# Moving the first head group's delta rule three steps later in a four-layer hybrid block

## The chip, the cores and the metric

One core of one Trainium2 chip runs the whole program once. The metric is device time in microseconds (us), from the host's request to its end; the profile's span runs from the first to the last instruction and is about 2 us shorter.

## The reference

Four layers over x of 256 tokens by 1024 channels, in fp32. Layers 1 and 2 are attention layers that the change doesn't touch. Layers 3 and 4 (`layer2` in the kernel) each do this, cut to what matters:

```
proj = rmsnorm(x) @ w_in            # q, k, v, z, b, a of the delta branch; q, k, v of the window branch; two gates
q, k, v = split(silu(conv4(q, k, v)))      # causal convolution over 4 tokens: the "taps"
q, k = l2norm(q) / sqrt(128), l2norm(k)    # 8 heads of 128
o = gated_delta_rule(q, k, v, g, beta)     # per head and chunk: a unit lower triangular solve
y_a = (rmsnorm(o) * silu(z)) @ w_up_dn
y_b = swa_sink(q, k, v) @ w_up_sw          # 16 heads, window of 128, sinks
x = x + rmsnorm((sigmoid(gate_a) * y_a + sigmoid(gate_b) * y_b) @ w_o)
x = x + rmsnorm(relu(rmsnorm(x) @ w_ff1)^2 @ w_ff2)
```

## The kernel before

**Projections.** TensorE (PE) multiplies in a split form: every weight piece `raw` (two rows of 128 input channels, 512 columns, 512 KB) is loaded by SyncE's queue (SP), copied by ScalarE (ACT) into `hi` (L290), and VectorE (DVE) writes the rest, `lo = raw - hi` (L291). Three matmuls per 128 channels then use hi and lo. `proj` (L318 to L320) makes token-major results, `proj_w` (L359 to L361) channel-major ones. Four split pieces and three raw ones are held; a piece's split is issued a half step after the piece four before it has been used, and the next raw load right behind it.

**The clock in the source.** Everything else is put between the matmuls by a clock that is written out by hand: `at(k, fn)` files work k steps ahead, and `tick(0.5)` after each half step first feeds a split and then issues what is due. A step is 128 input channels, so a projection of four pieces is 8 steps. Each engine then runs its own instructions in the order of issue.

**The delta branch in `layer2`.** The 8 heads are done in two groups `hh` of 4. Per group: `dn_qk` projects q and k (two `proj_w`), `dn_rest` files the delta rule, then come the gate's projection and that of v; the second group's q and k follow those, and then its own `dn_rest`, with the window branch (`swa`) between. Each convolution is filed by `into_conv`: ACT multiplies by one tap (L1001), DVE adds the three others with six instructions (L1004, "taps"), ACT takes tanh (L1008), DVE forms the silu (`emit`, L1021 for q and k, L1053 for v). For q and k, ACT squares it (L1029) and PE sums over channels into `pn` (L1027); for v PE transposes it (L1059) and DVE scales it into R (L1061).

**The delta rule as `dn_rest` files it**, from `start`, counted from the call:

- `decay_rows` at start - 3.2: a DMA on SP reads the decay sums `rw` from DRAM, spread over 128 partitions (512 KB, L1068).
- per head i, 2 steps apart from start - 1.5: `steps` (DVE, D from rw, L1074), exp and weigh (ACT, L1087, L1092), two `gram`s at start + 1.5 and + 1.7 (PE into a PSUM tile, L1096 and L1097; DVE multiplies by D, L1098), `pick` (POOL, L1113).
- at start + 9.5 `compact` (DVE, L1121); the 16x16 diagonal blocks go to DRAM and back in another layout (two DMAs on SP).
- at start + 15.1 to 18.1 the substitution on 64 partitions: two `eights` (DVE, L1149 and L1151), two `corner`s (DVE, L1164 and L1166, then L1159 and L1162); two DMAs again.
- at start + 21.7 and 22.7 `spread(1)` and `spread(0)` (DVE, L1169) make Xi, at start + 24.7 the doubling levels begin (`level_z` L1178, `level_y` L1188, `flip` L1107), then `solve`, `right` and `outputs`, the last at start + 41.8.

Grams, transposes, levels and the window branch's scores share three PSUM tiles of the tag `wk`; each is free again when ACT or DVE has read it. Each engine's queue keeps its order, so an instruction that waits holds up what is behind it.

Of the kernel before, what the change touches and what calls it, by code (L numbers as in the profile page):

```python
# [77 lines left out]
def body(ctx: ExitStack, tc: tile.TileContext, I, out, upto=None):  # L78
# [148 lines left out]
    clk = [0.0]  # L227
# [122 lines left out]
    def proj_w(lh, evac):  # L350

        acc = acc2()
        for c in range(8):
            if c % 2 == 0:
                hi, lo, n = piece()
            for m in range(4):
                a = acc[m // 2][:, (m % 2) * 256:(m % 2) * 256 + 256]
                sl = slice(m * 128, (m + 1) * 128)
                T.matmul(a, hi[:, c % 2, sl], lh[0][:, c, :], start=(c == 0 and m % 2 == 0), stop=False)  # L359
                T.matmul(a, hi[:, c % 2, sl], lh[1][:, c, :], start=False, stop=False)  # L360
                T.matmul(a, lo[:, c % 2, sl], lh[0][:, c, :], start=False, stop=(c == 7 and m % 2 == 1))  # L361
                if m == 3 and c % 2:
                    release()
                if m % 2:
                    if c == 7:
                        evac(acc[m // 2], m // 2)
                    tick(0.5)
# [518 lines left out]
    def layer2(l, last):  # L886
# [101 lines left out]
        def into_conv(m0, emit):  # L988

            def evac(acc, b):  # L990
                a = acc.rearrange("p (m t) -> p m t", m=2)
                w = cw[l]
                ha, hb = [sm.tile([128, 2, 256], F32, name="hcv", tag="hcv", bufs=4) for _ in range(2)]

                def tap(j, m):
                    c = 24 * j + m0 + 2 * b + m
                    return w[:, c:c + 1]

                def taps():
                    for m in range(2):  # L1000
                        S.activation(ha[:, m, :], a[:, m, :], AF.Copy, scale=tap(3, m))  # L1001
                    for d in (1, 2, 3):
                        for m in range(2):
                            V.scalar_tensor_tensor(ha[:, m, d:], a[:, m, :256 - d], tap(3 - d, m), ha[:, m, d:],  # L1004
                                                   op0=ALU.mult, op1=ALU.add)

                def silu():
                    S.activation(hb, ha, AF.Tanh)  # L1008

                for k, fn in ((0.4, taps), (4.2, silu), ((4.9, 4.7)[m0 // 4 % 2], lambda: emit(b, hb, ha))):  # L1010
                    at(k + b, fn)
            return evac

        def dn_qk(hh):
            dqk = qk_tile([2, 4, 256])
            dq, dk = dqk[:, 0], dqk[:, 1]
            pn = wk([128, 2, 2, 4], "pn", "o", 1)
            for qi, d in enumerate((dq, dk)):
                def emit(b, th, hcv, d=d, qi=qi):
                    x = d[:, 2 * b:2 * b + 2, :]  # L1020
                    V.scalar_tensor_tensor(x, th, 1.0, hcv, op0=ALU.add, op1=ALU.mult)  # L1021
                    sq = th

                    def norms():
                        for m in range(2):
                            for t in range(2):
                                T.matmul(pn[:, qi, t, 2 * b + m:2 * b + m + 1], sq[:, m, t * 128:(t + 1) * 128], ones,  # L1027
                                         start=True, stop=True)
                    at(1.1, lambda: S.activation(sq, x, AF.Square))  # L1029
                    at(3.4, norms)  # L1030
                proj_w(lh, into_conv(8 * qi + 4 * hh, emit))
            return dq, dk, pn
# [299 lines left out]
        m1, fins, end = [], [], 0.0  # L1332

        def gate(g):
            m1.append(t4k("tg"))
            proj(lh, into_tanh(m1[g], None))
# [3 lines left out]
        def swa(g):  # L1340
            q = qk_tile([8, 256], F32R)
            if g == 0:
                sw["lb"] = new_lh()
            y, evac = into_stack(q, None, rope2)
            proj(lh, evac)
            windowed(q, g, y)

        for hh in range(2):
            qkn = dn_qk(hh)
            emit_v, fin, end = dn_rest(hh, *qkn, max(10.5, end + -15.3 - clk[0]))  # L1350
            fins.append(fin)
            if hh:
                swa(0)
            gate(hh)
            if hh:
                swa(1)
            proj_w(lh, into_conv(16 + 4 * hh, emit_v))
# [169 lines left out]
    at(67.3, lambda: tab_load("bs", "nb16"))  # L1527
    at(8.9, vectors)
    steps = [layer1, layer1, layer2, layer2][:upto]
    for i, s in enumerate(steps):  # L1530
        s(i % 2, i == len(steps) - 1)
# [27 lines left out]
```

## Time and profile before

| | |
|---|---|
| median of 3 runs | 1730.53 us (1729.9 to 1733.3) |
| the profiled execution's own time | 1731.44 us |
| its span | 1729.5 us |
| mean granted TensorE clock | 0.995 of full speed |
| TensorE busy | 1699.3 us of the span (98%) |
| VectorE busy | 1171.5 us (68%) |
| ScalarE busy | 1000.7 us (58%) |

The time outside the span is 1.9 us. TensorE is busy nearly throughout, so the time is its work plus the stretches in which it stands. Shares over the whole span hide that these stretches stand close together; stages have to be read one by one.

### The profile page before, as it was taken

Reading aid. Unit: us, or ns where it says so; the run is one execution under the profiler, and the core shown is the slowest. Engines: PE = TensorE matmul, PEld = TensorE weight load, DVE = VectorE, ACT = ScalarE, POOL = GpSimd, SP = SyncE. Lnnn points to the kernel's source line nnn. Section 1 sums busy time; section 2 is a strip of 40 time slices with the busy share of each in tenths; the row PEclk is TensorE's granted clock in tenths of the full one; section 3 lists DMA queues with packets and bytes.
Section 4 is the critical chain, followed back from the end, with each engine's and each line's share of the span. In section 5 each row is a group of like instructions: output and inputs, shape, how many; then the busy total and the mean of one; then the engine's idle time right before and its main releaser. Section 6 shows DMA issues by size and latency. Waiting matters only on the chain.

```text
span 1729.5 us, 26895 instructions
## 1 busy us (share of the span) xinstructions
PE 1699.3 (98%) x9865; PEld 1482.8 (86%) x9865; DVE 1171.5 (68%) x2206; ACT 1000.7 (58%) x1787; POOL 259.4 (15%) x491
## 2 busy tenths in 40 slices
PE   9999999999999999998999999999999999999998
PEld 7788888888888888898898889998998898889997
DVE  6676866666678756878685676556778584775554
ACT  6666665466667554665676465445665666464443
POOL 1112320021123200420210000000320211010000
PEclk9999999999999999999999999999999999999999
DMA  6666465566555565555242546665554333556554
GB/s 220 192 177 177 153 186 162 173 197 178 169 171 166 164 195 170 165 167 143 83 117 86 195 158 187 191 195 172 164 166 140 88 103 98 195 160 199 183 182 142
DMA packets 158948, 282.27 MB, mean 163 GB/s; under 512 B 20576, under 2 KB 28512, under 8 KB 158816
## 3 DMA queue, kind: packets, MB, share of 16 engines
q1 hardware_dynamic: 157712, 277.57, 53.3%
q0 software_dynamic: 720, 2.62, 0.4%
q8 instruction: 78, 1.28, 0.3%
q14 instruction: 54, 0.44, 0.1%
q10 hardware_dynamic: 384, 0.35, 0.1%
HBM read 270.53 MB, written 1.59 MB: 157 GB/s over the span
## 4 chain that ended last, share of the span: by engine, by line
PE 49%; DVE 6%; issue 1%; ACT 1%; DMA 0%; POOL 0%; DVEq 0%; POOLq 0%; ACTq 0%
PE acc L320 6%; PE acc L318 6%; PE acc L319 6%; PE acc L359 5%; PE acc L360 4%; PE acc L361 4%; PE facc L318 3%; PE facc L319 3%; PE facc L320 3%; DVE lo L291 2%; DVE hcv L1004 1%; PE inv L1188 1%; PE inv L1178 1%; PE tp L377 1%; PE pg L1096 1%
## 5 line engine op out<-in xcount | busy, mean ns | idle before, releaser
L291 DVE TENSOR_TENSOR lo<-raw,hi 128x1024 fp32r<-128x1024 f32 (+2 forms) x505 | 617.0, 1228 | 367.8 <-ACT hi L290 354.6
L290 ACT ACTIVATE hi<-raw 128x1024 fp32r<-128x1024 f32 (+2 forms) x505 | 528.4, 1052 | 370.0 <-PE acc L320 158.6
L318 PE MATMUL acc<-hi,lhi 128*128 128x512 f32 (+1 forms) x1344 | 550.0, 409 | 1.3 <-ACT hi L290 1.3
L320 PE MATMUL acc<-hi,llo 128*128 128x512 f32 (+1 forms) x1344 | 525.4, 391 | 0.4 <-DVE llo L394 0.3
L319 PE MATMUL acc<-lo,lhi 128*128 128x512 f32 (+1 forms) x1344 | 523.9, 390 | 0.8 <-DVE lo L291 0.7
L320 PEld LDWEIGHTS acc<-hi,llo 128*128 128x128 f32 x1344 | 253.3, 188 | 57.5 <-DVE llo L394 3.5
L319 PEld LDWEIGHTS acc<-lo,lhi 128*128 128x128 f32 x1344 | 254.9, 190 | 41.5 <-DVE lo L291 2.5
L318 PEld LDWEIGHTS acc<-hi,lhi 128*128 128x128 f32 x1344 | 254.4, 189 | 39.9 <-ACT hi L290 1.6
L359 PE MATMUL acc<-lhi,hi 128*128 128x256 f32 x832 | 239.0, 287 | 0.0
L361 PE MATMUL acc<-lhi,lo 128*128 128x256 f32 x832 | 235.3, 283 | 0.0
L360 PE MATMUL acc<-llo,hi 128*128 128x256 f32 x832 | 235.2, 283 | 0.0
L359 PEld LDWEIGHTS acc<-lhi,hi 128*128 128x128 f32 x832 | 159.4, 192 | 1.2 <-issue 0.4
L360 PEld LDWEIGHTS acc<-llo,hi 128*128 128x128 f32 x832 | 159.4, 192 | 0.7
L361 PEld LDWEIGHTS acc<-lhi,lo 128*128 128x128 f32 x832 | 159.3, 191 | 0.0
L318 PE MATMUL facc<-hi,fh 128*128 128x512 f32 x256 | 99.8, 390 | 0.0
L319 PE MATMUL facc<-lo,fh 128*128 128x512 f32 x256 | 99.8, 390 | 0.0
L320 PE MATMUL facc<-hi,fl 128*128 128x512 f32 x256 | 99.6, 389 | 0.0
L516 ACT ACTIVATE ptS<-pt 128x384 f32<-128x384 f32 x80 | 39.3, 491 | 89.8 <-PE pt L514 89.3
L553 POOL TENSOR_SCALAR pf<-pss 128x1 f32<-128x1 f32 x8 | 3.7, 464 | 467.7 <-ACT pj L871 467.7
L507 DVE CUSTOM_DVE_ANT_0 s<-sc,tab 128x256 f32<-128x256 f32 x192 | 60.5, 353 | 10.7 <-PE sc L503 10.1
L1004 DVE SCALAR_TENSOR_TENSOR hcv<-acc,cw,hcv 128x255 f32<-128x255 f32 (+1 forms) x144 | 58.2, 477 | 2.1 <-ACT hcv L1001 2.0
L320 PEld LDWEIGHTS facc<-hi,fl 128*128 128x128 f32 x256 | 48.1, 188 | 10.1
(310 smaller groups left out, 2199.7 us busy)
## 6 DMA issues: line engine op xcount, KB each, us to landing
raw<-in_w_in_dram SPq DMA_DIRECT2D x271, 512.0 KB, 3.7
raw<-in_w_ff_dram SPq DMA_DIRECT2D x128, 512.0 KB, 4.2
raw<-in_w_proj_a_dram SPq DMA_DIRECT2D x16, 512.0 KB, 3.9
raw<-in_w_proj_b_dram SPq DMA_DIRECT2D x16, 512.0 KB, 3.8
raw<-in_w_out_dram SPq DMA_DIRECT2D x16, 512.0 KB, 3.8
raw<-in_w_up_sw_dram SPq DMA_DIRECT2D x16, 512.0 KB, 3.7
raw<-in_w_up_dn_dram SPq DMA_DIRECT2D x16, 512.0 KB, 3.6
raw<-in_w_o_dram SPq DMA_DIRECT2D x16, 512.0 KB, 3.8
```

Source lines behind the costliest of these rows:

```text
L290: S.activation(hi[:, c, :o], raw[:, c, :o], AF.Copy)
L291: V.tensor_tensor(out=lo[:, c, :o], in0=raw[:, c, :o], in1=hi[:, c, :o].bitcast(F32), op=ALU.subtract)
L318: T.matmul(a, lh[0][:, c, sl], hi[:, cc, :n], start=first, stop=False)
L319: T.matmul(a, lh[0][:, c, sl], lo[:, cc, :n], start=False, stop=False)
L320: T.matmul(a, lh[1][:, c, sl], hi[:, cc, :n], start=False, stop=last)
L359: T.matmul(a, hi[:, c % 2, sl], lh[0][:, c, :], start=(c == 0 and m % 2 == 0), stop=False)
L360: T.matmul(a, hi[:, c % 2, sl], lh[1][:, c, :], start=False, stop=False)
L361: T.matmul(a, lo[:, c % 2, sl], lh[0][:, c, :], start=False, stop=(c == 7 and m % 2 == 1))
L377: T.transpose(p[:, a, :], src[:, a * 128:(a + 1) * 128], ident)
L507: V.tensor_tensor_reduce(s[:, a:b], sc[:, a:b], bias[:, a:b], 1.0, FMIN, ALU.add, ALU.max, accum_out=mx[:, j:j + 1])
L516: S.activation(r, pt, AF.Copy)
L1004: V.scalar_tensor_tensor(ha[:, m, d:], a[:, m, :256 - d], tap(3 - d, m), ha[:, m, d:], op0=ALU.mult, op1=ALU.add)
```

## The change

For the first group (`hh` = 0) the delta rule starts at 13.5 steps behind the call and not at 10.5; the second group's floor stays 10.5.

```diff
         for hh in range(2):
             qkn = dn_qk(hh)
-            emit_v, fin, end = dn_rest(hh, *qkn, max(10.5, end + -15.3 - clk[0]))
+            emit_v, fin, end = dn_rest(hh, *qkn, max(10.5 if hh else 13.5, end + -15.3 - clk[0]))
             fins.append(fin)
```

Positions in steps from the first group's call of `dn_rest` (gate 0 to 8, v 8 to 16, second q 16 to 24, second k 24 to 32, window queries 32 to 40):

| | before | after |
|---|---|---|
| rw read on SP | 7.3 | 10.3 |
| D of head 0, 1, 2, 3 | 9, 11, 13, 15 | 12, 14, 16, 18 |
| grams of head 0, 1, 2, 3 | 12, 14, 16, 18 | 15, 17, 19, 21 |
| v's taps / silu / transposes (not moved) | 15.4, 16.9 / 19.9, 21.4 / 21.6, 23.1 | the same |
| compact | 20 | 23 |
| second q's taps / silu / norms (not moved) | 23.4, 24.9 / 27.7, 29.2 / 31.1, 32.6 | the same |
| eights | 25.6, 26.7 | 28.6, 29.7 |
| corners | 27.9, 28.6 | 30.9, 31.6 |
| second k's taps / silu / norms (not moved) | 31.4, 32.9 / 35.7, 37.2 / 39.1, 40.6 | the same |
| spread(1), spread(0) | 32.2, 33.2 | 35.2, 36.2 |
| first level_z | 35.2, 35.7 | 38.2, 38.7 |
| last outputs | 52.3 | 55.3 |

For the second group `end` is 52.3 before and 55.3 after, so `end - 15.3 - 32` is 5 or 8; both lie under 10.5, and the second group stands where it stood.

## Rows read from the trace of the kernel before

**Rows 1.** Windows of layer 3: length, then busy us (instructions) per engine, clock, DMA.

```profile
764.00:786.00 22.00, 21.61 (x173) 21.10 (x172) 21.59 (x37) 14.28 (x26) 7.55 (x7) 1.00 0.49 126
786.00:812.00 26.00, 21.77 (x151) 19.25 (x150) 24.07 (x52) 11.96 (x18) 0.00 (x0) 1.00 0.50 134
812.00:864.00 52.00, 51.14 (x342) 46.04 (x340) 30.89 (x69) 32.72 (x76) 11.96 (x24) 1.00 0.33 98
```

**Rows 2.** Waits of TensorE from 735 to 960 us (layer 3): us, times, longest.

```profile
PE pn L1027 <- ACT hcv L1029: 2.7, 2, 1.5
PE inv L1178 <- DVE Xi L1169: 1.5, 2, 1.1
...
PE tp L1059 <- DVE hcv L1053: 0.4, 1, 0.4
```

**Rows 3.** Groups of TensorE, 1300 to 1335 us (layer 4): busy, mean ns, idle before.

```profile
L1027 PE MATMUL pn<-ones,hcv 128*128 128x1 f32 x24 | 3.1, 248 | 2.7 <-ACT hcv L1029 2.7
```

**Rows 4.** Timeline of TensorE: fifteen matmuls between norms and levels, layers 3 and 4.

```profile
800.99 0.72 PE L1027 MATMUL pn<-ones,hcv 128*128 128x1 f32 x5 [1.45 <-ACT hcv L1029]
...
801.91 0.48 PE L318 MATMUL acc<-hi,lhi 128*128 128x512 f32 x1
...
805.19 0.39 PE L320 MATMUL acc<-hi,llo 128*128 128x512 f32 x1
...
1317.53 0.49 PE L318 MATMUL acc<-hi,lhi 128*128 128x512 f32 x1
...
1322.43 0.40 PE L320 MATMUL acc<-hi,llo 128*128 128x512 f32 x1
```

**Rows 5.** Windows: proj_w alone in layer 3, and the slow stretch of layer 4.

```profile
785.00:794.00 9.00, 9.00 (x77) 9.00 (x77) 8.69 (x26) 4.24 (x7) 0.00 (x0) 1.00 0.56 143
...
1316.00:1324.00 8.00, 7.38 (x33) 6.23 (x34) 7.71 (x16) 4.28 (x8) 0.00 (x0) 0.79 0.64 177
```

**Rows 6.** Timeline of SP's queue where the decay rows are read.

```profile
752.48 0.37 SPq L279 DMA_DIRECT2D raw<-in_w_in_dram  x1
752.94 0.42 SPq L1068 DMA_DIRECT2D rw<-gr  x1
```

**Rows 7.** Timeline of VectorE in v's projection: start, us, instruction, idle time before it.

```profile
758.39 0.75 DVE L1074 SCALAR_TENSOR_TENSOR D<-rw,cs,tab 128x256 f32<-128x256 f32 x2 [1.82 <-DMA rw<-gr]
...
759.59 1.21 DVE L291 TENSOR_TENSOR lo<-raw,hi 128x1024 fp32r<-128x1024 f32 x1
```

**Rows 8.** Timeline of ScalarE: the split at step 10, and the first weigh.

```profile
757.40 1.06 ACT L290 ACTIVATE hi<-raw 128x1024 fp32r<-128x1024 f32 x1 [2.08 <-PE acc L360]
...
762.55 0.80 ACT L1092 ACTIVATE D<-D,cj 128x256 f32<-128x256 f32 x2 [2.85 <-POOL cj L1047]
```

**Rows 9.** Timeline of TensorE: two grams of one head at step 16, and what follows.

```profile
768.54 0.60 PE L1096 MATMUL pg<-qk 128*128 128x256 f32 x2
...
769.12 0.36 PE L359 MATMUL acc<-lhi,hi 128*128 128x256 f32 x1
```

**Rows 10.** Groups of VectorE from 764 to 812 us: busy us, mean ns.

```profile
L1098 DVE TENSOR_TENSOR AT<-pg,D 128x384 f32<-128x384 f32 x4 | 2.2, 553 | 0.0
...
L1121 DVE TENSOR_REDUCE Xi<-Y 128x128 f32<-128x1024 f32 x1 | 2.0, 1955 | 0.0
```

**Rows 11.** Timeline of VectorE from the substitution to the first spread.

```profile
790.82 0.15 DVE L1149 TENSOR_TENSOR Y<-Y 64x2 f32<-64x2 f32 x1
...
792.30 1.22 DVE L291 TENSOR_TENSOR lo<-raw,hi 128x1024 fp32r<-128x1024 f32 x1
...
795.48 0.68 DVE L1164 TENSOR_TENSOR Y<-Y 64x512 f32<-64x512 f32 x1
...
797.93 1.04 DVE L1159 TENSOR_TENSOR Y<-Y 64x512 f32<-64x512 f32 x1
...
799.60 0.67 DVE L1021 SCALAR_TENSOR_TENSOR qk<-hcv 128x512 f32<-128x512 f32 x1
...
801.70 2.43 DVE L1004 SCALAR_TENSOR_TENSOR hcv<-acc,cw,hcv 128x255 f32<-128x255 f32 x6 [0.29 <-ACT hcv L1001]
```

## The prediction

> **What bounds the kernel now.** The page's busy times come first: TensorE (PE) is busy nearly all the span, so the change can win only where PE stands and lose only where it makes PE stand. Next I read windows of layer 3 around the moved work. Over the second group's q and k projections PE loses 4 us in one window, and there the busy engine is VectorE (DVE): 21.6 of 22 us, then 24.1 of 26 [rows 1]. In the 52 us behind them DVE is busy 31 us and PE hardly stands. So this stretch, 764 to 812 us, is DVE's, and DVE's queue has to be followed in order.
>
> PE's waits name the places: 2.7 us before the norms of q (for a square behind DVE's silu), 1.5 us before the first levels (for the spreads), 0.4 us before v's transposes [rows 2]. Layer 4 has the same 2.7 us before the norms [rows 3] and nearly nothing before the levels, but the fifteen matmuls ahead of these run from 1317.53 to 1322.43, where layer 3 needs 801.91 to 805.19 [rows 4]: 4.90 against 3.28 us. The granted clock was 0.79 in that window [rows 5], so part of it ran at 1.2 and not 2.4 GHz, just behind PE's waits for the norms; that cost 1.6 us.
>
> What can be won is thus, per layer: 4.6 us of waits in layer 3, plus about 0.16 us for each of five waits, because a matmul's shown 0.39 us overlaps the next one's start 0.23 us later [rows 4]: 5.4. In layer 4 I take 2.7 for the norms, some 0.5 for the two small waits, 0.6 for the overlap and 1.6 for the clock: 5.4 again.
>
> **What the change does.** It removes and adds no instruction. Per layer it moves five DMAs of SP's queue, 8 grams, 4 picks of POOL (which has 7.6 us of work in 22 [rows 1], so nothing), the substitution, spreads, levels and outputs. The second group stays.
>
> *The norms.* Before, q's first silu stands behind both eights and the second behind both corners too; after, the first has none of them ahead of it and the second only the first eights. Eights cost 1.48 us each (790.82 to 792.30), the corners 1.32 (795.48 to 797.93, less the lo of 1.13 between) and 1.67 (797.93 to 799.60) [rows 11]. That takes DVE work of 3.0 and 4.5 us from in front of the two silus, and the 1.2 and 1.5 us that PE waited there are gone, if DVE is not later for another reason.
>
> *That other reason: the decay rows.* D of head 0 needs rw. Before, SP issues rw at 752.94, right behind a raw load that waited for the split of step 6 [rows 6]; D starts 5.4 us later, at 758.39, with DVE idle for 1.82 us and a split's lo queued behind it (759.59) [rows 7]. After, rw is filed for step 10.3. In the same half step the feed has just issued the split of step 10 and the raw load behind it, so rw stands behind a load that waits for this split's lo. Its hi starts at 757.40 [rows 8], lo then runs from 758.5 to 759.7, the load goes at 759.7 and rw at 760.2. With the 5.4 us of the row it is there at 765.5. D is due at step 12, about 760.1 on PE, and now there is no split ahead of it to fill the gap: DVE stands from 759.7 to 765.5, and the next lo and all else queue behind D.
>
> Bounds of that price: the shortest wait is that of before, 1.8 us, the longest 5.8. I take 5.6, as the length of the read is a row of the same transfer and the order in the queue is fixed by the source. The Trainium skill (DMA: Bandwidth & Descriptors, Anatomy of one DMA — SWDGE (gpsimd) path) gives a DMA as 2.0 us plus its bytes by 436 GB/s, for another path than this queue's; as an estimate for 512 KB that is 3.2 us, where the row shows 5.4, and by the page the sum below would be about 2 us per layer smaller.
>
> *DVE from there*, with start-to-start times (about 0.09 us under the shown ones): lo 1.13, six taps 2.34, D 0.66, a gram's product 0.47, silu or R 0.60, compact 1.87 [rows 7, 10, 11]. From 765.5: D, lo, D reach 768.0; the next lo waits for its hi (1.06 on ScalarE, behind D's exp and weigh, which take some 1.3 with the weigh's shown 0.80 [rows 8]) to 768.5 and runs to 769.6; two products 770.6; v's taps 772.9; D and lo 774.7; v's taps 777.1; the product of head 1's first gram 777.5.
>
> *PE at the grams.* Step 16 was at 768.54 with four grams more behind it than after, so it comes at about 767.3. A gram is 0.57 us [rows 9], with the switch 0.65; a half step of proj_w is 6 matmuls at 0.117, 0.72 with rounding [rows 5]. Seven half steps and three grams later PE stands before head 2's second gram, step 19.5, at 774.3. The three PSUM tiles then hold head 1's two grams and head 2's first, none read yet, since DVE does v's taps. The first is free at 777.5. A new wait of 3.2 us; if the DMA wait stayed 1.8 us it would be nothing.
>
> *PE at the levels.* From 777.5 DVE has, up to and with spread(1): 9 lo (10.2 us), 24 taps in four sixes (9.4), five products (2.4), one D (0.7), compact (1.9), four silus and two R (3.6), both eights (3.0), both corners (3.0), one spread (0.6): 34.6 us, so to 812.1. PE from 777.5 needs 0.65 for the gram, 25 half steps of proj_w to step 32 (18.0), two grams and two transposes of four small matmuls, these put at 0.45 (2.2 in all), norms 0.9 twice [rows 4], and 13 half steps of proj (0.70 each by rows 4, 9.1): 31.7, so it is there at 809.2. A wait of 2.9 us, and some 0.7 more for spread(0), before which DVE does a silu and a lo. The DMAs between compact, eights, corners and spread have about the same DVE work over them as before and are hidden, by a margin near 1 us.
>
> *Behind it.* The levels now stand three steps deeper in the window branch's scores and share the three PSUM tiles with them and the second group's grams. DVE has slack there [rows 1]; from nothing to 1.5 us per layer, the longest single wait now [rows 2]; I take 0.6, nearer to nothing for that slack.
>
> **Sum per layer:** - 5.4 + 3.2 + 2.9 + 0.7 + 0.6 = + 2.0 us; two layers + 4.0. The new waits are twice as long as the ones behind which the clock fell, so I keep one stretch at half clock, + 1.6: + 5.6. On the profiled execution's 1731.4 that is 1737.0; the median of the runs shown lies 0.9 lower, so 1736.1.
>
> **Rivals.**
>
> *Faster: the silus' move is all that counts.* If rw is there when DVE gets to D, and DVE reaches spread(1) by 809.2, PE's old waits go and no new ones come: - 10.8, + 1.2 behind, about + 1 left at the grams: - 8.6, 1722. For it: 7.3 us really leave the front of the silus. Against: DVE's total work to the spreads is the same, and its list would have to be 2.9 us (8%) shorter as well.
>
> *No change.* The read takes 3.4 us instead of 5.4: the gram's wait falls to 1.2 and the layers come out at 0.0 each, the clock at nothing to 1.6: 1730.5 to 1732.1. The same follows if the spreads' wait is 2 us shorter.
>
> *Slower still: half clock behind every new long wait.* Two per layer at 1.6 instead of one in all: + 4.0 + 6.4: 1741. The row of layer 4 is for it [rows 5], the unchanged 1.00 behind the equal waits of layer 3 [rows 1] against it; and a slow PE behind the gram is partly given back at the levels, where it would wait anyhow. The Trainium skill (TensorE: Matmul & The Clock Gate, Why this matters for your kernels) holds that gaps between bursts of matmuls send the clock back to half; layer 4 agrees (0.79), layer 3 does not.
>
> *The change isn't what it says.* In program order it is, but for the second corner (31.6), which passes k's first taps (31.4).
>
> **How the numbers follow.** A measurement here tells about 0.2% (3.5 us) from no change. Forecast (1733 to 1739.5): 0.52. Half clock everywhere: 0.14. No change: 0.21. Faster: 0.13. Of the forecast's part a little lies within 0.2%, so faster 0.12, same 0.25, slower 0.63. The range leaves out most of the faster case and the end of the slow one: 1729.5 to 1741.
>
> **What would show it.** DVE idle for some 5 to 6 us before the first D, released by the rw read, with that read issued behind a raw load near 760; PE waiting about 3 us at L1096 for a product and about 3 us at L1178 for the spread; no waits before q's norms. Wrong would be: D on time, or TensorE's waits at the levels under 1 us; or DVE taking up its backlog faster than its rows add up.

## The result and the profile after

The changed kernel takes 1746.68 us (median of 5 runs, 1744.73 to 1751.55), the kernel before 1730.53: a ratio of 1.0091, with a 95% interval of 1.0081 to 1.0102. It is slower by 16 us, where 5.6 were forecast; the time lies outside the range. The profiled execution took 1748.69 us, its span is 1746.6, its mean granted clock 0.992.

The windows that answer to [rows 1], each set 2 us later because the profiled execution comes to layer 3 some 2.7 us later:

```profile
766.00:788.00 22.00, 19.31 (x138) 18.54 (x138) 19.06 (x36) 12.26 (x23) 2.94 (x4) 0.92 0.45 130
788.00:814.00 26.00, 24.96 (x175) 23.07 (x174) 25.52 (x54) 13.32 (x21) 0.43 (x2) 1.00 0.45 121
814.00:866.00 52.00, 47.74 (x304) 42.38 (x304) 32.77 (x72) 30.19 (x62) 11.25 (x20) 0.97 0.39 109
```

TensorE now gains in the middle window (24.96 busy of 26, where it had 21.77), and loses ahead of it (19.31 of 22) and behind it (47.74 of 52). The waits of TensorE say behind what; those of layer 3, answering to [rows 2]:

```profile
PE inv L1178 <- DVE Xi L1169: 3.9, 1, 3.9
PE pg L1096 <- DVE LT L1098: 2.7, 1, 2.7
...
PE pt L514 <- ACT e L1295: 0.9, 1, 0.9
PE tp L452 <- ACT ptS L516: 0.8, 1, 0.8
...
PE pt L514 <- DVE mx L507: 0.3, 1, 0.3
PE inv L1188 <- DVE LA L1098: 0.2, 1, 0.2
```

The norms' line is gone, as forecast, and so are the waits of v's transposes. In their place stand one wait for a gram's product and one for the spread, and four small ones behind step 40. Layer 4 has the same list with 4.2 and 3.0 in the first two lines. New less old waits come to 3.9 us in layer 3 (8.8 against the 4.6 of [rows 2] and 0.3 more in the line below, of the kernel before) and 5.9 in layer 4 (9.4 against 3.5).

```profile
PE tp L452 <- DVE mx L507: 0.3, 1, 0.3
```

The clock comes on top. Windows of 20 us around the three stretches of these layers in which the changed kernel's granted clock fell (the third figure from the end is the clock):

```profile
770.00:790.00 20.00, 17.31 (x125) 16.65 (x124) 18.58 (x34) 11.01 (x21) 2.94 (x4) 0.91 0.47 132
810.00:830.00 20.00, 16.11 (x95) 14.10 (x94) 14.21 (x29) 8.29 (x13) 3.39 (x10) 0.91 0.58 155
1330.00:1350.00 20.00, 15.71 (x88) 13.32 (x86) 14.79 (x26) 8.85 (x13) 2.94 (x8) 0.91 0.54 160
```

Over the middle 10 us of each the clock is 0.83, which is 1.7 us lost. They lie behind the wait for the product, behind the spread's in layer 3 and behind the spread's in layer 4. The kernel before lost 1.7 us in one such place, that of [rows 5] (0.79 over 8 us). That makes 3.4 us more.

Lateness of the changed kernel's profiled execution, by the start of the same projection matmul in both traces:

| us late at step | 8 | 16 | 24 | 32 | 40 | 56 | 64 |
|---|---|---|---|---|---|---|---|
| layer 3 | 2.8 | 0.9 | 6.6 | 5.0 | 4.1 | 8.0 | 9.8 |
| layer 4 | 9.9 | 8.0 | 12.9 | 11.5 | 11.1 | 15.0 | 16.7 |

Most of the 2.8 us at the start of it (2.3) arose in layer 1, at 50 to 60 us, where the clock of this one execution fell to 0.83; no instruction there was changed, and the execution is 2.0 us above its median. The two changed layers add 7.0 and 6.9, together 13.8: waits of 3.9 and 5.9 and clock of 3.4 are 13.2 of these. Part of the 5.6 us between steps 40 and 64 is no loss but the levels' own matmuls, which now stand behind step 40.

### The profile page after: what moved, and what is told of

Its sections match the earlier page's. It is cut to its first block, busy times and chain, and to the rows that moved or that the text cites. A ratio compares the mean times of both kernels' runs of the same rounds, so it can differ in the third digit from the quotient of the medians.

```text
span 1746.6 us, 26888 instructions
## 1 busy us (share of the span) xinstructions
PE 1704.7 (98%) x9865; PEld 1486.7 (85%) x9865; DVE 1171.2 (67%) x2206; ACT 1000.1 (57%) x1787; POOL 246.6 (14%) x491
## 4 chain that ended last, share of the span: by engine, by line
PE 47%; DVE 7%; ACT 3%; DMA 2%; issue 1%; POOL 0%; DVEq 0%; POOLq 0%; ACTq 0%; SPq 0%
PE acc L320 5%; PE acc L318 5%; PE acc L319 5%; PE acc L359 4%; PE acc L360 4%; PE acc L361 4%; PE facc L318 3%; PE facc L319 3%; PE facc L320 3%; DVE lo L291 3%; DVE hcv L1004 2%; PE inv L1188 1%; PE inv L1178 1%; ACT hi L290 1%; PE tp L377 1%
## 5 line engine op out<-in xcount | busy, mean ns | idle before, releaser
L507 DVE CUSTOM_DVE_ANT_0 s<-sc,tab 128x256 f32<-128x256 f32 x192 | 60.3, 351 | 11.1 <-PE sc L503 10.5
```

Of the source, the lines that this page charges most:

```text
L507: V.tensor_tensor_reduce(s[:, a:b], sc[:, a:b], bias[:, a:b], 1.0, FMIN, ALU.add, ALU.max, accum_out=mx[:, j:j + 1])
```

## The experiments

**The read of the decay rows.** First the changed kernel with this read filed 0.3 steps sooner, at 10.0, so that SP issues it ahead of the raw load:

```diff
-            at(k - 3.2, decay_rows)
+            at(k - (3.2 if hh else 3.5), decay_rows)
```

> The changed kernel (1746.7 us) with one edit: the decay rows are read 0.3 step earlier, at step 10.0 and not 10.3, so that SP issues the read ahead of the raw load of step 10 and not behind it. Theory A (the read behind the raw load is the main cause): VectorE no longer idles near 6 us before the first D, TensorE's wait at the grams (2.7 and 3.0 us) goes, and with it the stretch at half clock behind it: 1737 to 1740. Theory B (the levels' and spreads' later place is the main cause): the gram's wait goes, but the time comes back at the spreads: 1744 to 1747.

Then the kernel before with only its read 1.4 steps later, at 8.7, behind a raw load:

```diff
-            at(k - 3.2, decay_rows)
+            at(k - (3.2 if hh else 1.8), decay_rows)
```

> The kernel before (1730.5 us) with one edit: the first group's decay rows are read at step 8.7 and not 7.3, behind the raw load of step 8; nothing else is moved. Theory A: D comes some 4 us later, TensorE waits at the grams and at v's transposes, 1737 to 1741. Theory B: a read that is late by itself is made up before the spreads, 1730 to 1733.

Measured: the first 1740.58 us (ratio 1.0054, 1.0039 to 1.0069), 6.1 below the changed kernel; the second 1739.73 (1.0049, 1.0034 to 1.0064), 7.1 above the 1732.61 of the kernel before in the same runs. In the changed kernel, SP's queue and then VectorE's:

```profile
759.36 3.51 SPq L279 DMA_DIRECT2D raw<-in_w_in_dram  x2
762.96 0.42 SPq L1068 DMA_DIRECT2D rw<-gr  x1
```

```profile
761.25 1.23 DVE L291 TENSOR_TENSOR lo<-raw,hi 128x1024 fp32r<-128x1024 f32 x1 [1.39 <-ACT hi L290]
767.52 0.75 DVE L1074 SCALAR_TENSOR_TENSOR D<-rw,cs,tab 128x256 f32<-128x256 f32 x2 [5.04 <-DMA rw<-gr]
```

The load waits for the lo that ends at 762.5, the read is issued right behind it, and VectorE stands for 5.04 us. With the read ahead of the load, D waits half as long, and the line of L1096 is gone from layer 3:

```profile
760.73 0.75 DVE L1074 SCALAR_TENSOR_TENSOR D<-rw,cs,tab 128x256 f32<-128x256 f32 x2 [2.31 <-DMA rw<-gr]
```

```profile
PE inv L1178 <- DVE Xi L1169: 4.3, 1, 4.3
PE pt L514 <- ACT e L1295: 0.9, 1, 0.9
...
PE tp L452 <- ACT ptS L516: 0.8, 1, 0.8
```

In the kernel before the late read makes the same hole (D behind 5.17 us of idle time), although nothing else has moved. Its trace shows other losses behind the hole, though: two waits at the grams of 1.4 and 1.8 us and 1.6 us before v's transposes in each layer, less waiting at the norms and levels of layer 3, and a long stretch at half clock there:

```profile
PE pn L1027 <- ACT hcv L1029: 1.9, 2, 1.2
PE tp L1059 <- DVE hcv L1053: 1.6, 2, 0.8
PE pg L1096 <- DVE LT L1098: 1.4, 1, 1.4
```

```profile
800.00:810.00 10.00, 9.30 (x31) 7.33 (x32) 9.68 (x17) 4.09 (x7) 0.00 (x0) 0.56 0.56 133
810.00:820.00 10.00, 10.00 (x63) 8.72 (x62) 6.67 (x15) 4.72 (x9) 0.00 (x0) 0.93 0.46 136
```

All its waits together are 0.3 and 3.2 us longer than before in layers 3 and 4, and the clock takes 5.1 us more in layer 3 (1.00 in the kernel before, below). So a read that is filed behind a load costs 6 to 7 us by the medians (6.4 and 8.5 by the ratios). In the changed kernel this answers to two layers of waits at the grams (5.7 us) and one stretch at half clock (1.7); alone in the kernel before, more than half of it is clock in the execution shown. The other 8 us of the loss (1740.58 less 1732.61) have another place: the wait for the spread is undiminished without the hole.

**The substitution, and the levels.** The kernel before with the first group's compact, eights, corners, spreads and all behind them three steps later, its read and grams where they were; and with only the levels and what follows them three steps later:

```diff
-            k += 9.5
+            k += 9.5 if hh else 12.5
             at(k, compact)
```

> The kernel before with D and grams where they were, and all from compact on (substitution, spreads, levels, outputs) three steps later. Theory A: the norms' waits go (2.7 us per layer), a wait of about 3 us comes at the spreads, and the levels cost 0 to 2 us more behind: 1729 to 1735. Theory B: nearly the whole loss of the change, 1740 to 1747.

```diff
-                at(k + 3.1 + 0.5 * t, lambda t=t: flip("Xi", "Y", t))
-            k += 2.5
+                at(k + 3.1 + 0.5 * t + (0 if hh else 3), lambda t=t: flip("Xi", "Y", t))
+            k += 2.5 if hh else 5.5
```

> The kernel before with only the levels, solves and outputs three steps later; the spreads stay at 32.2 and 33.2. Theory A: the waits before the levels go (1.5 us in layer 3, 0.2 in layer 4), the levels lie deeper in the window branch and cost up to 2 us per layer: 1729 to 1734. Theory B (the levels' later place costs most): 1737 to 1744.

The first took 1738.46 us (1.0041, 1.0026 to 1.0056), between its two expectations, with the spread's wait at 3.8 us in both layers and none at the norms: this part alone makes the spread's wait and takes the norms' away. The second took 1735.01 (1.0013, 1.0002 to 1.0023), 2.4 us above the kernel before and again between the two: the spread's waits are gone, 2.7 us at the norms remain, and the small waits behind step 40 are all there. So these do not come from the substitution. The line of the spread in the first, and that of the norms in the second, both of layer 3:

```profile
PE inv L1178 <- DVE Xi L1169: 3.8, 1, 3.8
```

```profile
PE pn L1027 <- ACT hcv L1029: 2.7, 2, 1.5
```

These runs also bound what the grams' own later place costs. The first experiment (the whole change with the read ahead) and the substitution alone differ in D and the grams: 1740.58 against 1738.46, 2.1 us, with intervals that overlap.

In the changed kernel the chain of work that ended last runs through the last two DMAs of the substitution to the spread:

```profile
809.88 0.69 DVE Y L1162
810.63 1.94 DMA dg<-Y
812.59 3.41 DMA Y<-dg
816.02 0.70 DVE Xi L1169
```

VectorE is done with the second corner at 810.6, has six taps and two lo over the DMAs and then stands 0.86 us for the second of them. The DMAs that were taken as hidden by about 1 us were short of cover by as much: the second corner now comes behind k's first taps (806.46 to 808.79 on VectorE), so these 2.3 us no longer lie over the DMAs.

**The last outputs.** The kernel before with nothing moved but the last outputs, from 52.3 to 55.3:

```diff
-            at(k + 4.1, lambda: outputs(1))
+            at(k + (4.1 if hh else 7.1), lambda: outputs(1))
```

> The kernel before with one edit: only the first group's last outputs (8 matmuls for 4 heads twice over, one copy and four squares on ScalarE, the root on POOL) are issued at step 55.3 and not 52.3; everything else stands. Theory A2 (behind step 40 the cost is that these 1.8 us of ScalarE work come between the window queries' two evictions and in front of a head's exp, so that TensorE waits 0.9 us for the exp and 0.8 us for a transpose's tile): both waits appear, about 1.9 us per layer, plus 3 to 4 us in all. Theory B2 (the levels among the scores and the second group's grams cost it): nothing, within 1.5 us of the kernel before.

1736.96 us (1.0028, 1.0017 to 1.0039): both waits are there, 0.9 and 0.8 us in each layer, without those of 0.3 and 0.2, which thus come with the levels; and from step 56 to 64 the kernel falls 1.77 us behind in both. ScalarE's timeline, first of this kernel, then of the kernel before:

```profile
874.91 0.60 ACT L446 ACTIVATE tok<-acc 128x512 f32<-128x512 f32 x1 [3.50 <-PE o L1215]
...
875.77 0.61 ACT L1216 ACTIVATE R<-o 128x512 f32<-128x512 f32 x1
...
877.60 0.58 ACT L446 ACTIVATE tok<-acc 128x512 f32<-128x512 f32 x1
...
879.02 0.49 ACT L1295 ACTIVATE e<-s,nm 128x256 f32<-128x256 f32 x1
```

```profile
870.08 0.60 ACT L446 ACTIVATE tok<-acc 128x512 f32<-128x512 f32 x1 [1.42 <-PE acc L320]
...
871.10 0.60 ACT L446 ACTIVATE tok<-acc 128x512 f32<-128x512 f32 x1
...
872.54 0.50 ACT L1295 ACTIVATE e<-s,nm 128x256 f32<-128x256 f32 x1
```

The copy and the squares of the outputs stand between the two evictions (copies out of PSUM, L446) of the second window query's projection: from the first of these to exp it is 4.11 us and not 2.46, and TensorE's transposes of the probabilities (L514) wait 0.88 us. Two layers of it are 3.5 of the 5.3 us by which the median lies above the kernel before beside it (1731.65), where 3 to 4 were expected. The profiled execution also has longer stretches at half clock at the norms (below), in work that is not changed; how much of the median they make is open.

Then, with the read ahead, the changed kernel with the last outputs sooner (54.7) or later (55.8):

```diff
-            at(k + 4.1, lambda: outputs(1))
+            at(k + (4.1 if hh else 3.5), lambda: outputs(1))
```

> The changed kernel with the rw read ahead of its load (as in the first experiment, 1740.6 us), and with the first group's last outputs filed 0.6 steps earlier (54.7 instead of 55.3), so that ScalarE's copy and squares of them stand ahead of tok's two evictions and 0.86 us sooner ahead of exp. Theory: the waits pt<-e (0.9 us) and tp<-ptS (0.8) behind step 40 come from where these outputs stand on ScalarE; they fall to under half, so about 0.8 to 1.7 us per layer come back: 1737 to 1739. Rival: they come from the levels' depth in the window branch, wherever the last outputs stand: 1740.6 within 0.7, the two waits unchanged.

> The same with the last outputs 0.5 steps later (55.8 instead of 55.3): behind tok's second eviction, but still ahead of the next exp on ScalarE. Theory: the second rope is on time, so tp<-ptS goes or shrinks (0.8 us per layer), but exp stays late or gets later, so pt<-e stays at 0.9 or grows by up to 0.7: 1738.5 to 1741.5. Rival (depth of the levels alone): 1740.6 within 0.7 with both waits unchanged.

They took 1739.81 us (1.0046, 1.0031 to 1.006) and 1741.59 (1.0058, 1.0044 to 1.0071), against 1740.58 for the first experiment. Sooner, the wait of 0.9 for exp is gone, but a new one of 0.4 comes (values for ptS, L520), and the 0.8 us before the second transposes of tok stay; later, all stay and the 0.4 comes too. So half of the theory held: exp's wait hangs on where the outputs stand. The 0.8 us do not go away by half a step either way, and three times with overlapping intervals don't rank the places. The traces do: from step 56 to 64 the three fall 1.2 (sooner), 1.8 and 2.6 us (later) behind the kernel before, alike in both layers.

**Filling the wait.** The first experiment with 16 more matmuls per layer ahead of the levels, whose results nothing reads:

```diff
+            def fill():
+                d = ps.tile([128, 512], F32, name="acc", tag="acc", bufs=4)
+                for _ in range(16):
+                    T.matmul(d, lh[0][:, 0, 0:128], lh[0][:, 0:2, :], start=True, stop=True)
+            if not hh:
+                at(k - 0.51, fill)
```

> The version with the decay rows read ahead (some 8 us slower than the kernel before) and 16 more matmuls of 512 columns, whose result nobody reads, right ahead of the first levels, where TensorE waits 4.3 us for the spread. They take 3.7 us. Theory A3 (that wait sends TensorE to half clock for one or two stretches behind it, which cost some 3 us in layer 3 and 1.5 in layer 4): with the wait filled the granted clock stays at 1.00 behind it and the kernel is 2 to 4.5 us faster than the same without the filling. Theory B3 (the half clock behind the wait is hidden by other waits): the same time, or 1 us slower.

1738.82 us (1.0036, 1.0023 to 1.0049): with some 3.6 us more to do per layer, TensorE ends sooner by the medians, 1.8 us, less than the 2 to 4.5 expected, and the two intervals overlap. The profiled executions agree: from step 8 to 64 the filled one falls 2.8 us behind the kernel before in each layer, the other 4.7 and 4.0. The wait for the spread falls to 1.2 and 1.3 us, in two parts each, and the clock stays up where it fell without the fill. The 20 us around the spread in layer 3, first filled, then not:

```profile
800.00:820.00 20.00, 18.76 (x106) 15.44 (x105) 15.43 (x28) 9.35 (x14) 2.94 (x8) 1.00 0.58 163
```

```profile
800.00:820.00 20.00, 15.66 (x80) 13.35 (x79) 13.48 (x25) 8.84 (x13) 2.93 (x8) 0.83 0.54 154
```

Unfilled, 0.17 of 20 us is 3.4 us of clock, nearly as much as the wait of 4.3 itself.

**One step instead of three.** The kernel before with its levels one step later; with its substitution one step later and the levels one more; the same again on another occasion; and the whole delta rule one step later (a start of 11.5), with the read at step 8.0, ahead of its load. The lines of the second version, of which the first has only those behind the dots:

```diff
-            k += 9.5
+            k += 9.5 if hh else 10.5
...
-                at(k + 3.1 + 0.5 * t, lambda t=t: flip("Xi", "Y", t))
-            k += 2.5
+                at(k + 3.1 + 0.5 * t + (0 if hh else 1), lambda t=t: flip("Xi", "Y", t))
+            k += 2.5 if hh else 3.5
```

> The kernel before with only the levels, solves and outputs one step later (first levels at 36.2 and 36.7). Theory A: the wait before the levels (1.5 us in layer 3) goes, the last outputs at 53.3 stay clear of the window queries' evictions: 0.5 to 2.5 us faster than the kernel before. Theory B2 (any delay of the levels costs): 0.5 to 1.5 us slower.

> The kernel before with compact, substitution and spreads one step later and levels, solves and outputs two. Theory A: the second norms wait (1.5 us per layer) goes because one corner less stands ahead of q's second silu, the wait before the levels stays under 2 us, the last outputs at 54.3 are just clear: 1 to 4 us faster than the kernel before. Theory B: 1 to 4 us slower, as a third to two thirds of the change.

> The same kernel as the eighth experiment (the kernel before with the first group's substitution one step later and its levels one further step, 1729.62 us, ratio 0.9988), timed once more beside the kernel before on another occasion, because 2 us is no more than one or two stretches at half clock. Theory (waits really gone: q's norms wait 1.3 us once where the kernel before waits twice, and the clock has less to fall behind): ratio 0.998 to 0.9995, granted clock 0.997 or more. Rival (the first time it happened to draw runs with few such stretches): ratio 0.9995 to 1.0015, granted clock 0.995 or less.

> The changed kernel with a start of 11.5, so the whole delta rule of the first group moves one step instead of three, and the rw read at 8.0, ahead of its load. Theory (the loss is made of three places that three steps overrun: the read behind a load, the spreads behind VectorE, the last outputs among the evictions; none is overrun at one step, where the outputs stand at 53.3): no wait for D, none over 1.5 us at L1178, norms' wait about 1.3 us shorter or gone: 1728 to 1732. Rival (each step of delay costs its share, a third of the 9 us that three steps cost with the read ahead): 1733 to 1735.

| | us | ratio | interval |
|---|---|---|---|
| levels 1 | 1733.30 | 1.0008 | 0.9996 to 1.0020 |
| substitution 1, levels 2 | 1729.62 | 0.9988 | 0.9978 to 0.9997 |
| the same again | 1729.65 | 0.9990 | 0.9982 to 0.9999 |
| all 1, read ahead | 1735.92 | 1.0018 | 1.0010 to 1.0027 |

The levels alone can't be told from no change. The second version is the one that beats both kernels, by 2 us and twice; the repeat's interval still reaches into the range of its rival (0.9995 and more). Waits of its layer 3 in the first of the two:

```profile
PE pn L1027 <- ACT hcv L1029: 1.3, 1, 1.3
PE pt L514 <- DVE llo L384: 0.7, 1, 0.7
PE tp L452 <- DVE mx L507: 0.6, 1, 0.6
...
```

Half of the norms' wait is gone and in layer 3 the spread's too, without a new one over 0.4 us. Layer 4 is less clear: the spread's wait there is 1.4 us (0.2 before) in the first of the two and gone in the second, which has 0.8 us before v's transposes instead (0.3 before). From step 8 to 64 the two profiled executions gain 2.9 and 1.3 us over both layers. Their granted clock is 0.998 and 0.997, but over all the runs of this version it lies, one of 0.947 aside, from 0.992 to 0.998, as that of the kernel before does; so a gain in clock is not shown.

The whole rule one step later is slower than either expectation: its layer 3 waits 2.7 us for the spread and 1.6 at the norms. The levels at one step alone bring three new waits of 0.4 to 0.7 us in the window branch that are not there at two, and the same three are here, in both layers. Besides the levels' step it differs from the second version in the read, D and the grams; which of these makes the rest no run separates. Its median is 2.9 us above its own profiled execution; that one came to layer 3 some 1.7 us ahead of the kernel before, where nothing was changed, and lost 2.4 us in the two layers.

## Why the prediction was too small

**Right in kind.** The read is issued behind a raw load (762.96 in a layer that began 2.8 us late, so 760.2, as forecast); VectorE stands 5.04 us where 5.6 were taken, because the read took 4.6 us from issue to D and not the 5.4 of [rows 6, 7]. The Trainium skill (DMA: Bandwidth & Descriptors, Anatomy of one DMA — SWDGE (gpsimd) path) would give an estimate of 3.2 us for this size on another path; the trace does not agree, here with 4.6. TensorE's wait at the grams is 2.7 and 3.0 us (3.2 forecast), that at the spreads 3.9 and 4.2 (2.9 and 0.7 forecast), and the norms wait no more. The experiments on single parts show the late read as a cause of waits at the grams (without it they go; alone it makes them, with 1.4 and 1.8 us), and the substitution's place as the cause of the spread's wait and of the norms' end.

**The spread's wait, right for nearly the reason given.** The forecast set both engines at the gram, at 777.5, and took the wait from what each has to do from there; by that reckoning it doesn't hang on the hole at D, and without the hole it is indeed 3.8 and 4.3 us. The list for VectorE held 34.6 us and took 36.9 (779.71 to 816.63), of which 0.86 is the stand for the last DMA, which was to be hidden, and 0.68 one for a gram; that for TensorE held 31.7 and took 33.0, with 1.7 of clock that the forecast hadn't put there. The two errors partly cancel, so the close sizes are in part luck.

**The step that failed: "Behind it ... I take 0.6".** It measured 1.9 us net in each layer (0.9, 0.8, 0.3 and 0.2, less 0.3 of before). I had looked for slack on VectorE and at the three PSUM tiles; the place was ScalarE's queue, where the moved outputs stand between two evictions and ahead of an exp. The bound given with it, 1.5 us, was too low as well. Over two layers that is 2.6 us more than forecast.

**The second, and the largest: "I keep one stretch at half clock".** There are three in these layers, where the kernel before had one: 5.1 us less 1.7, not 1.6 less 1.6. That is the rival "half clock behind every new long wait" but for one of its four places, the gram's in layer 4. Its own time, 1741, was too low by the other two steps. That such a stretch costs time is borne out for the spread's by the filled wait; for the gram's it is read from one execution.

**The third: what is won.** Only the listed waits came back, 4.6 us in layer 3 and 3.2 in layer 4, besides the clock of layer 4; the 0.16 us added for the overlap of each wait and the bit more in layer 4 (9.2 in all without the clock) left no trace.

In sum over both layers, forecast and measured in the profiled executions: won - 9.2 and - 7.8; grams + 6.4 and + 5.7; spreads + 7.2 and + 8.1; behind step 40 + 1.2 and + 3.8; clock 0 net and + 3.4. These are + 5.6 and + 13.2. The rest up to 16.2 is not assigned; the medians of the kernel before, from one chip and occasion to another, went from 1730.53 to 1732.61. By medians the same loss falls into 6.1 us for the read behind its load (1746.68 to 1740.58), 2.1 for D and the grams (to 1738.46), 5.9 for all from compact on (to 1732.61), and 2.1 between the two occasions.

## What to carry to other kernels

A step that is filed later passes not only work on the engines but the points in the queues at which other instructions wait: write down for each moved instruction, the last ones too, what stands directly ahead of it and behind it on its own queue, ScalarE's evictions and SP's loads before all. A wait of TensorE of about 4 us should be priced with the half clock behind it: each of the ten waits for the spread of 3.8 to 4.4 us in these traces has 1.7 or 3.4 us of it behind, while of three waits of 2.7 to 3.0 us one has 1.7 and two have none. And a move that pays at one step can lose at three: here what gained was the substitution by one step and the levels by two, with the grams and their read left in place.

## What the runs showed of the hardware

**The same wait, with and without half clock.** The experiment with the last outputs changes nothing ahead of step 52, so its norms in layer 3 are those of the kernel before. TensorE's wait before the first norm is alike, 1.23 and 1.22 us, but the clock is not. The kernel before, then the experiment:

```profile
800.00:820.00 20.00, 17.46 (x106) 14.80 (x107) 15.15 (x30) 12.04 (x20) 0.70 (x2) 1.00 0.51 137
```

```profile
800.00:820.00 20.00, 19.38 (x93) 16.18 (x94) 16.41 (x30) 8.82 (x16) 0.00 (x0) 0.74 0.48 131
```

By the clock that is 5.2 us lost or nothing, with the second wait even shorter (0.62 against 1.45 us). The loss in time is smaller: from step 32 to 40 this execution falls 1.6 us behind the kernel before, as a slower TensorE comes later to its second wait and to the levels, and finds the one shorter and the 1.5 us before the others gone. The Trainium skill (TensorE: Matmul & The Clock Gate, Why this matters for your kernels) has gaps between bursts, longer ones than these, send the clock to half; the first trace agrees with that, and in the second the clock fell although its waits were no longer. A single execution therefore doesn't show what a short wait costs; the runs of the kernel before lie 6.4 us apart beside one experiment (1729.13 to 1735.57).

**VectorE stands while GpSimd runs.** In the experiment with the sooner outputs the second group's first eights fall under GpSimd's rotary step on tok (L433 to L436). Timelines of VectorE and of GpSimd:

```profile
877.03 0.33 DVE L1149 TENSOR_TENSOR Y<-Y 64x2 f32<-64x2 f32 x1
877.40 0.15 DVE L1151 TENSOR_REDUCE Y<-Y 64x2 f32<-64x2 f32 x1
877.58 0.33 DVE L1149 TENSOR_TENSOR Y<-Y 64x8 f32<-64x8 f32 x1
```

```profile
877.03 0.32 POOL L435 TENSOR_TENSOR rb<-tok,ss 128x64 f32<-128x64 f32 x1
877.43 0.47 POOL L436 TENSOR_TENSOR tok<-ra,rb 128x128 f32<-128x128 f32 x1
```

The product over 64x2 takes 0.33 us where [rows 11] has 0.15 for the same one, and ends when GpSimd's instruction does; the reduction, with one input, is not slowed. The Trainium skill (SBUF — State Buffer, SBUF: two separate sides) has an instruction of VectorE with two inputs from SBUF and one of GpSimd that reads SBUF exclude each other for a whole instruction; the rows agree. It is a candidate for the 0.8 us before tok's second transposes, as VectorE's max stands behind these eights; no run here separates it.
